# A decoder layer on one core: the up half is built in the fourth product's bank, the late splits come one plain unit later, and the bank copies have an earlier place in the queue

## The chip, the core and the metric

The kernel runs on one core of one Trainium2 chip. TensorE multiplies matrices into the eight banks of PSUM, ScalarE and VectorE work on PSUM and on SBUF, GpSimd (POOL) starts software DMAs here, among them those that add to what lies at the target, and SyncE (SP) starts plain loads. Each engine takes its instructions in the order of its queue; semaphores make one engine wait for another. The metric is the device time of one launch in microseconds, the median of several runs.

## The reference

One layer of a hybrid decoder for 256 tokens, width 2048, in float32: a half-step SwiGLU, a mixer (differential attention and a matrix-memory LSTM after one combined projection), an output projection, a second half-step SwiGLU, and a final RMSNorm. Nearly all of the work is in the weight products:

```python
def swiglu(h, w_gate, w_up, w_down):
    return (jax.nn.silu(h @ w_gate) * (h @ w_up)) @ w_down
...
x = x + 0.5 * swiglu(rmsnorm(x, ffn1_norm[l]), ffn1_w_gate[l], ffn1_w_up[l], ffn1_w_down[l])
h = rmsnorm(x, mix_norm[l])
a_q, a_k, a_v, m_q, m_k, m_v, m_o, m_i, m_f = jnp.split(h @ w_in[l], split_idx, axis=-1)
...
x = x + jnp.concatenate([y_a, y_b], axis=-1) @ w_out[l]
x = x + 0.5 * swiglu(rmsnorm(x, ffn2_norm[l]), ffn2_w_gate[l], ffn2_w_up[l], ffn2_w_down[l])
```

The inner width of each SwiGLU is 5632. All weights come from HBM once, 393 MB of reads.

## The kernel before, in words

**Float32 by three products.** A weight tile is split on ScalarE into a rounded part (`hi`, a cast, L131) and on VectorE into the rest (`lo`, a subtraction that follows the cast, L132). The activations are split in the same way beforehand. A product is then three matmuls (`mms`): L173 and L174 with the high weights, L176 with the low ones. The split tiles lie in a ring of four pairs of buffers (pool `wsp`, `bufs=4`). One entry in the list `splits` is one unit: mostly two 128-row blocks of weights, that is six or twelve matmuls.

**Pairs.** Two column chunks of 512 columns are worked through together by the class `Paired`: `wa` and `wb`, which for the FFN are gate and up of the same chunk, and elsewhere two neighbouring chunks. The result has four banks: two halves of the tokens times two chunks. The inner dimension goes in blocks of 256 rows. The first `ns` blocks of a pair use a scheme of Strassen's kind with seven products of 128 x 128 x 512 in place of eight; the others are plain units (`plain`). There are 45 pairs: `ns` is 5 in the FFN's gate and up chunks (2 in the first pair of all), 3 or 1 in the down chunks, 2 for the first projection pair, 3, 4, 4, 4, 3 in the mixer and 3 in the output projection.

**One pair, in order of its products.** `leading` loads three weight blocks per block (`raw`), multiplies A1 into the bank `self.x`, copies that bank to the seeded bank N11 (L444, through `copied`), adds weight blocks on VectorE (L448), multiplies S1 into the bank `self.d`, and then adds `raw[2]` to `raw[0]`, by a DMA from POOL (L455), or on VectorE where `by_dma` is false (L457), as in the down chunks. `sums` copies `self.d` to SBUF (`ds`, L488), multiplies S2 onto `self.x`, starts a DMA that adds another weight block to `raw[0]` (L494), copies `self.x` to the seeded bank N12 (L495), multiplies the first late weights (`bare`) into N11, multiplies S3 onto `self.x`, copies it to the seeded bank N21 (L499), and on VectorE turns N12 and `self.x` into `ds` minus themselves (L502). The copies of L495 and L499 run on ScalarE as L464; TensorE may go on writing into `self.x` only when the copy has read it. `second` works through the plain units of `wa` into N11 and N21, and after each plain unit one late split (`both`): of `raw[0]` and `raw[2]`, with the products B2 into N21 and S4 into N12. Its banks are then evacuated as the first chunk. `third` runs the plain units of `wb` into N12 and `self.x`, in turn with the next pair's `leading` (`Chain.run`).

**What sets the order.** A planner orders each engine's queue by priority and by what it expects to be ready. Weight splits have priority `AHEAD`, copies and evacuations 40 more (`soon`). Beside that, `ahead_of_splits(i, ins)` puts an instruction into a list, and `split_weights` makes the split that comes `SLACK` = 4 units later follow it on ScalarE (list 0) or VectorE (list 1). That is a bound: the copy can stand earlier, not later. The weight loads of the next pair reuse the `raw` buffers (pool `wr`, five) once the late splits have read them; plain and late units load through five buffers of their own (`rawp`) on SP.

**Banks.** PSUM has eight: three in the ring `acc` (`bank()`, also used by the mixer's small products), three seeded (N11, N12, N21), two for transposes.

Of the kernel before, what the change touches and what calls it, by code (L numbers as in the profile page):

```python
# [21 lines left out]
KD = D // P  # L22
# [30 lines left out]
SEEDED = N11, N12, N21 = "n11", "n12", "n21"  # L53
# [6 lines left out]
def tile_trunk_layer(ctx: ExitStack, tc: tile.TileContext, x, xt, par, bias_if, lamv, fnorm,  # L60
# [10 lines left out]
    ps_acc = ctx.enter_context(tc.tile_pool(name="ps_acc", bufs=3, space=PSUM))  # L71
# [24 lines left out]
    def seeded(which):  # L96
        return ps_acc.tile([P, CW], F32, tag=f"acc{which}", name=nm(f"acc{which}"), bufs=1)
# [46 lines left out]
    def ahead_of_splits(i, ins):  # L144
        queued[i].append((len(splits), ins))

    def split_weights(src, hi, lo):
        made = split(src, hi, lo)
        for late, q in zip(made, queued):
            while q and len(splits) >= q[0][0] + SLACK:  # L150
                after(late, q.pop(0)[1])
        return made
# [237 lines left out]
    class Paired:  # L390

        def __init__(self, xp, wa, wb, nk, ns, w0=0, queue=nc.gpsimd, by_dma=True):

            self.queue, self.by_dma = queue, by_dma
# [40 lines left out]
        def leading(self):  # L435
# [3 lines left out]
            for js in self.twos:  # L439
# [3 lines left out]
                if js[-1] == self.ns - 1:  # L443
                    self.n11 = self.copied(N11)  # L444
# [15 lines left out]
        def copied(self, which):  # L460

            t = seeded(which)[:, 0:self.n]
            with soon():
                ahead_of_splits(0, nc.scalar.copy(t, self.x))  # L464
            return t
# [18 lines left out]
        def sums(self):  # L484

            with soon():
                ds = wk("ds")[:, 0:self.n]
                ahead_of_splits(0, nc.scalar.copy(ds, self.d))  # L488
# [6 lines left out]
            self.n12 = self.copied(N12)  # L495
# [3 lines left out]
            self.n21 = self.copied(N21)  # L499
            with soon():  # L500
                for t in (self.n12, self.x):
                    ahead_of_splits(1, nc.vector.tensor_tensor(out=t, in0=ds, in1=t, op=ALU.subtract))  # L502
# [14 lines left out]
        def second(self):  # L517

            def both(j):
                t = self.split_two([self.raws[j][:, 0:3:2, :]])  # L520
                mms([self.job(self.n21, j, B2, t, 0, False, False, True), self.job(self.n12, j, S4, t, 1, False, False, True)])

            for i in range(max(self.ns, len(self.rest))):
# [6 lines left out]
                if i < self.ns:  # L530
                    both(i)
# [18 lines left out]
        def accs(self):  # L550
            return [p[:, self.off:] for p in (self.n12, self.x)]
# [40 lines left out]
    def ffn(chain, xp, rstd, wg, wu, wd, finish, first=None):  # L592
# [21 lines left out]
        for part, (n, ns) in enumerate(zip(PARTS, NP_DOWN)):  # L614
            hid = {}
            for c in range(n):
                half, end = inner(hid, c, ns)
                if done + c == 0 and first is not None:
# [3 lines left out]
                    stream = units(au, xp, wu[0], KD, banks=[functools.partial(seeded, N12), bank])  # L622
# [588 lines left out]
```

## Time and profile before

| What | Value |
|---|---|
| median of 3 runs | 1818.47 us (1815.88 to 1821.22) |
| profiled execution, its own time | 1818.1 us |
| its span, first to last instruction | 1816.4 us |
| mean granted TensorE clock | 0.997 |
| DMA packets | 443.22 MB, mean 244 GB/s |

The profile shows one execution. A row of the timeline has the start in us from the beginning of the span, the duration, the engine, the line of the kernel, the operation, what it writes and reads, and in brackets how long the engine had been idle and what released it. PE stands for TensorE's matmuls, PEld for its weight loads, ACT for ScalarE, DVE for VectorE. A row of the list of waits has the waiting group, the one that released it, the idle time in all, the number of waits and the longest. A row of the groups has, after the bar, busy time and mean duration in ns, then the idle time before and its releasers. A row of the stretches has, for each stretch, the busy time of PE, PEld, DVE, ACT and POOL with the number of instructions, the granted clock, the DMA share and GB/s.

### The profile page before, as it was taken

What the parts mean: (1) busy time and instruction counts of PE and PEld (TensorE: products, weight loads), DVE (VectorE), ACT (ScalarE), POOL (GpSimd) and SP (SyncE); (2) the same over time, 40 slices, a digit from 0 to 9 for tenths busy, and PEclk for the clock granted to TensorE, in tenths of its full rate; (3) what the DMA queues carried; (4) which work ended last, traced back from release to release, by engine and by line L of the source; (5) the groups of instructions that cost most, each with busy time, mean ns of one, the idle gap of its engine ahead of it and who ended that gap; (6) DMA issues with size and microseconds to landing.
All of it is one profiled execution on the core that took longest, in us unless ns stands there. A gap on an engine that the chain in (4) does not pass through costs nothing. (4 is left out here: it accounts for less than half of the span.)

```text
span 1816.4 us, 24465 instructions
## 1 busy us (share of the span) xinstructions
PE 1772.5 (98%) x7955; PEld 1443.7 (79%) x7955; DVE 1560.5 (86%) x2074; ACT 1261.0 (69%) x1939; POOL 471.1 (26%) x669
## 2 busy tenths in 40 slices
PE   9899999999999999999999999999999999999997
PEld 7688778788887887987788788788788788878886
DVE  6788888889988989796788899899887889988997
ACT  7566766767676767677576777776776767676765
POOL 0031431333243322112222112131432333143310
PEclk9999999999999999999999999999999999999999
DMA  9887998999899986687877678997998999899974
GB/s 337 249 212 229 249 265 269 216 282 259 270 241 270 264 279 197 183 258 208 232 208 208 169 228 225 240 277 240 255 274 271 240 275 265 240 261 278 259 256 122
DMA packets 161857, 443.22 MB, mean 244 GB/s; under 512 B 18273, under 2 KB 19585, under 8 KB 161473
## 3 DMA queue, kind: packets, MB, share of 16 engines
q0 software_dynamic: 82256, 204.67, 47.6%
q1 hardware_dynamic: 78464, 234.90, 36.8%
q10 hardware_dynamic: 1008, 2.09, 0.3%
q8 instruction: 62, 1.02, 0.2%
q14 instruction: 67, 0.54, 0.1%
HBM read 393.48 MB, written 2.10 MB: 218 GB/s over the span
## 5 line engine op out<-in xcount | busy, mean ns | idle before, releaser
L131 ACT CAST wh<-raw 128x512 fp32r<-128x512 f32 (+1 forms) x845 | 568.9, 705 | 307.2 <-DVE raw L448 144.2
L132 DVE TENSOR_TENSOR wl<-raw,wh 128x512 fp32r<-128x512 f32 (+1 forms) x845 | 646.9, 793 | 112.8 <-ACT wh L131 97.6
L132 DVE TENSOR_TENSOR wl<-rawp,wh 128x1024 fp32r<-128x1024 f32 (+3 forms) x324 | 387.6, 1199 | 81.6 <-ACT wh L131 78.7
L131 ACT CAST wh<-rawp 128x1024 fp32r<-128x1024 f32 (+3 forms) x324 | 334.0, 1033 | 112.3 <-PE accn L174 59.0
L173 PE MATMUL accn<-wh,xt 128*128 128x512 f32 (+2 forms) x888 | 350.5, 397 | 2.1 <-ACT accn L464 1.3
L174 PE MATMUL accn<-wh,xt 128*128 128x512 f32 (+2 forms) x888 | 343.7, 389 | 0.0
L173 PE MATMUL acc<-wh,xs 128*128 128x512 f32 (+2 forms) x712 | 280.0, 394 | 28.3 <-ACT accn L464 21.4
L174 PE MATMUL acc<-wh,xs 128*128 128x512 f32 (+2 forms) x712 | 275.6, 388 | 0.0
L176 PE MATMUL accn<-wl,xt 128*128 128x512 f32 (+2 forms) x888 | 258.0, 389 | 0.2
L176 PE MATMUL acc<-wl,xs 128*128 128x512 f32 (+2 forms) x712 | 233.0, 388 | 0.0
L455 POOL DMA_DIRECT2D raw<-raw x128 | 110.8, 873 | 465.6 <-DVE wl L132 379.2
L173 PE MATMUL accn<-wh,xs 128*128 128x512 f32 (+1 forms) x576 | 225.8, 393 | 2.7 <-ACT wh L131 2.3
L174 PE MATMUL accn<-wh,xs 128*128 128x512 f32 (+1 forms) x576 | 223.9, 390 | 0.0
L448 DVE TENSOR_TENSOR raw<-raw 128x1024 f32<-128x1024 f32 x168 | 199.7, 1216 | 0.4
L173 PEld LDWEIGHTS accn<-wh,xt 128*128 128x128 f32 x888 | 166.1, 188 | 42.0 <-ACT accn L464 5.6
L176 PEld LDWEIGHTS accn<-wl,xt 128*128 128x128 f32 x888 | 165.9, 188 | 37.2 <-DVE wl L132 3.5
L174 PEld LDWEIGHTS accn<-wh,xt 128*128 128x128 f32 x888 | 166.8, 188 | 31.8
L173 PEld LDWEIGHTS acc<-wh,xs 128*128 128x128 f32 x712 | 133.8, 188 | 70.3 <-ACT accn L464 34.9
L176 PE MATMUL accn<-wl,xs 128*128 128x512 f32 (+1 forms) x576 | 182.6, 390 | 0.7 <-DVE wl L132 0.5
L176 PEld LDWEIGHTS acc<-wl,xs 128*128 128x128 f32 x712 | 133.1, 188 | 31.4 <-DVE wl L132 3.8
L174 PEld LDWEIGHTS acc<-wh,xs 128*128 128x128 f32 x712 | 133.9, 188 | 25.9 <-DVE xs L132 0.4
L173 PEld LDWEIGHTS accn<-wh,xs 128*128 128x128 f32 x576 | 108.7, 189 | 26.6 <-ACT wh L131 3.2
(236 smaller groups left out, 2112.7 us busy)
## 6 DMA issues: line engine op xcount, KB each, us to landing
rawp<-in_wd_dram SPq DMA_DIRECT2D x96, 512.0 KB, 5.5
raw<-in_wg_dram POOLq DMA_DIRECT2D x182, 256.0 KB, 7.2
raw<-in_wu_dram POOLq DMA_DIRECT2D x80, 512.0 KB, 8.6
rawp<-in_wu_dram SPq DMA_DIRECT2D x74, 512.0 KB, 6.6
rawp<-in_wg_dram SPq DMA_DIRECT2D x70, 512.0 KB, 5.6
raw<-raw POOLq DMA_DIRECT2D x126, 256.0 KB, 4.1
rawp<-in_win_dram SPq DMA_DIRECT2D x44, 512.0 KB, 5.6
late<-in_wg_dram SPq DMA_DIRECT2D x41, 512.0 KB, 9.6
```

The source lines that it names most:

```text
L131: return (nc.scalar.copy(hi, src), nc.vector.tensor_tensor(out=lo, in0=src, in1=hi.bitcast(F32), op=ALU.subtract))
L132: nc.vector.tensor_tensor(out=lo, in0=src, in1=hi.bitcast(F32), op=ALU.subtract))
L173: nc.tensor.matmul(acc, lh, rh, start=first, stop=False, skip_group_check=on)
L174: nc.tensor.matmul(acc, ll, rh, start=False, stop=False, skip_group_check=on)
L176: nc.tensor.matmul(acc, lh, rl, start=False, stop=last, skip_group_check=on)
L448: nc.vector.tensor_tensor(out=raw[:, 0:2, :], in0=raw[:, 0:3:2, :], in1=raw[:, 1:2, :].to_broadcast([P, 2, n]), op=ALU.add)
L455: nc.gpsimd.dma_start(raw[:, 0, :], raw[:, 2, :], accum_op=ALU.add)
```

## The change

The seeded bank N12 is dropped and the ring `acc` gets a fourth bank. In `sums` the second copy of `self.x` goes to an SBUF tile (`us`), and VectorE subtracts it at once from `self.d`, in place; `self.d` is then what N12 was, for S4 and for the plain units of `wb`. The copies made by `copied` (N11, `ds`, `us`, N21) get a bound of three units instead of four. In `second` the late split of a block comes after the plain unit that follows, not after its own, so the loop has up to one more turn. Pairs with up to three blocks add `raw[2]` on VectorE instead of by DMA. The first chunk's up half takes both banks from the ring.

```diff
-SEEDED = N11, N12, N21 = "n11", "n12", "n21"
+SEEDED = N11, N21 = "n11", "n21"
...
-    ps_acc = ctx.enter_context(tc.tile_pool(name="ps_acc", bufs=3, space=PSUM))
+    ps_acc = ctx.enter_context(tc.tile_pool(name="ps_acc", bufs=4, space=PSUM))
...
-    def ahead_of_splits(i, ins):
-        queued[i].append((len(splits), ins))
+    def ahead_of_splits(i, ins, slack=SLACK):
+        queued[i].append((len(splits) + slack, ins))
...
-            while q and len(splits) >= q[0][0] + SLACK:
+            while q and len(splits) >= q[0][0]:
...
-            self.queue, self.by_dma = queue, by_dma
+            self.queue, self.by_dma = queue, by_dma and ns > 3
...
-                    self.n11 = self.copied(N11)
+                    self.n11 = self.copied(self.x, seeded(N11))
...
-        def copied(self, which):
-            t = seeded(which)[:, 0:self.n]
+        def copied(self, src, t):
+            t = t[:, 0:self.n]
             with soon():
-                ahead_of_splits(0, nc.scalar.copy(t, self.x))
+                ahead_of_splits(0, nc.scalar.copy(t, src), SLACK - 1)
             return t
...
-            with soon():
-                ds = wk("ds")[:, 0:self.n]
-                ahead_of_splits(0, nc.scalar.copy(ds, self.d))
+            ds = self.copied(self.d, wk("ds"))
...
-            self.n12 = self.copied(N12)
+            us = self.copied(self.x, wk("us"))
+            with soon():
+                ahead_of_splits(1, nc.vector.tensor_tensor(out=self.d, in0=self.d, in1=us, op=ALU.subtract))
...
-            self.n21 = self.copied(N21)
+            self.n21 = self.copied(self.x, seeded(N21))
             with soon():
-                for t in (self.n12, self.x):
-                    ahead_of_splits(1, nc.vector.tensor_tensor(out=t, in0=ds, in1=t, op=ALU.subtract))
+                ahead_of_splits(1, nc.vector.tensor_tensor(out=self.x, in0=ds, in1=self.x, op=ALU.subtract))
...
-            for i in range(max(self.ns, len(self.rest))):
+            for i in range(max(self.ns + 1, len(self.rest))):
...
-                if i < self.ns:
-                    both(i)
+                if 0 < i <= self.ns:
+                    both(i - 1)
...
-            return [p[:, self.off:] for p in (self.n12, self.x)]
+            return [p[:, self.off:] for p in (self.d, self.x)]
...
-                    stream = units(au, xp, wu[0], KD, banks=[functools.partial(seeded, N12), bank])
+                    stream = units(au, xp, wu[0], KD, banks=[bank, bank])
```

More of the change, by code (lines that the diff above doesn't have):

```diff
@@ L520, in both @@
                 t = self.split_two([self.raws[j][:, 0:3:2, :]])
-                mms([self.job(self.n21, j, B2, t, 0, False, False, True), self.job(self.n12, j, S4, t, 1, False, False, True)])
-            for i in range(max(self.ns, len(self.rest))):
+                mms([self.job(self.n21, j, B2, t, 0, False, False, True), self.job(self.d, j, S4, t, 1, False, False, True)])
+            for i in range(max(self.ns + 1, len(self.rest))):
                 aside(side)
```

## The prediction

> **What bounds the kernel now.** I read the page first, then the list of who waited for whom on the matmul queue, then that list by stage, then the ScalarE and matmul timelines around single waits.
>
> ```profile
> span 1816.4 us, 24465 instructions
> ```
> ```profile
> PE 1772.5 (98%) x7955; PEld 1443.7 (79%) x7955; DVE 1560.5 (86%) x2074; ACT 1261.0 (69%) x1939; POOL 471.1 (26%) x669
> ```
> ```profile
> PE acc L173 <- ACT accn L464: 21.4, 27, 2.5
> ```
> ```profile
> PE accn L173 <- ACT accn L464: 1.7, 4, 0.6
> ```
>
> TensorE is the bound: it is busy for 98% of the span and idle for 1816.4 - 1772.5 = 43.9 us. The change leaves its matmuls as they are (one start-up matmul fewer, while the first weights are still on their way), so only idle time can go. Most of that has one cause: L464, the ScalarE copy of a product's bank, lets TensorE go on only after 21.4 + 1.7 = 23.1 us of idle time in 31 waits. The idle figure is a little short. Rows of matmuls overlap:
>
> ```profile
> 225.40 0.50 PE L173 MATMUL acc<-wh,xs 128*128 128x512 f32 x1 [1.53 <-ACT accn L464]
> 225.74 0.40 PE L174 MATMUL acc<-wh,xs 128*128 128x512 f32 x1
> 225.97 0.39 PE L173 MATMUL acc<-wh,xs 128*128 128x512 f32 x1
> ```
>
> In step, a matmul starts 0.23 us after the one before (225.74, 225.97), though its row is 0.39 long. A wait therefore costs its idle time plus about 0.16 us. By stage, each row from its own stretch (48 to 73 us, 73 to 690, 690 to 740, 740 to 1090, 1090 to the end):
>
> ```profile
> PE acc L173 <- ACT wh L131: 3.9, 2, 2.6
> PE acc L173 <- ACT accn L464: 2.5, 1, 2.5
> ```
> ```profile
> PE acc L173 <- ACT accn L464: 6.8, 9, 1.5
> ```
> ```profile
> PE accn L173 <- ACT accn L464: 1.3, 3, 0.6
> ```
> ```profile
> PE acc L173 <- ACT accn L464: 1.8, 2, 0.9
> ```
> ```profile
> PE acc L173 <- ACT accn L464: 4.2, 6, 1.5
> ```
> ```profile
> PE acc L173 <- ACT accn L464: 6.2, 9, 1.4
> ```
>
> **Copies ahead in the queue, and the order of the late splits.** A copy waits for its turn on ScalarE. Its bound is the fourth unit split after its place in the program; now it is the third. With four weight buffers, the third cannot start before the last unit that feeds the copy has been read, so a copy in front of it holds ScalarE for a few tenths of a us at most, and the split it passes is needed two or three units later (a unit of six matmuls is 6 x 0.23 = 1.36 us). I cost that delay at nothing; with no cover it is one copy, 0.58 us, per pair. What a copy gains depends on what stood before it. Three kinds, ScalarE rows. Five blocks in the middle of an FFN stage, the copy behind the casts of all five S3 blocks:
>
> ```profile
> 394.98 2.70 ACT L131 CAST wh<-raw 128x512 fp32r<-128x512 f32 x5
> 397.58 0.58 ACT L464 COPY accn<-acc 128x512 f32<-128x512 f32 x1
> ```
>
> It passes the fifth cast and starts 0.52 us earlier (2.70 for five, overlapped). Four blocks in the mixer, where it passes a whole late unit, about 0.95 us:
>
> ```profile
> 929.04 1.05 ACT L131 CAST wh<-late 128x1024 fp32r<-128x1024 f32 x1
> 929.99 0.59 ACT L464 COPY accn<-acc 128x512 f32<-128x512 f32 x1
> ```
>
> Three, two or one block, where it stands behind a late split that itself waits for the accumulating DMA:
>
> ```profile
> 157.05 1.05 ACT L131 CAST wh<-raw 128x1024 fp32r<-128x1024 f32 x1 [0.90 <-DMA raw<-in_wd_dram]
> 158.01 1.04 ACT L131 CAST wh<-rawp 128x1024 fp32r<-128x1024 f32 x1
> 158.96 0.58 ACT L464 COPY accn<-acc 128x512 f32<-128x512 f32 x1
> ```
>
> Here the change in `second` helps as well: the plain unit now comes before that late split, and the bound of three lets the copy go before it; 0.90 + 1.0 us are gained, more than the stall. A fourth kind gains nothing: after a down stage the copy already stands before S3's fifth cast, so the new bound does not bind.
>
> ```profile
> 354.48 2.20 ACT L131 CAST wh<-raw 128x512 fp32r<-128x512 f32 x4
> 356.56 0.60 ACT L464 COPY accn<-acc 128x512 f32<-128x512 f32 x1
> ```
> ```profile
> 1630.58 0.50 PE L173 MATMUL acc<-wh,xs 128*128 128x512 f32 x1 [1.17 <-ACT accn L464]
> ```
>
> ```profile
> 439.96 0.50 PE L173 MATMUL acc<-wh,xs 128*128 128x512 f32 x1 [0.28 <-ACT accn L464]
> ```
>
> ```profile
> 830.29 0.50 PE L173 MATMUL acc<-wh,xs 128*128 128x512 f32 x1 [0.26 <-ACT accn L464]
> ```
>
> There are six long ones, the first at 225.40, the last at 1630.58, about 7.3 us of idle time together, and four short ones of 0.28, the first at 439.96; the row at 830.29 is of a four-block pair of the mixer. The sum by stage, idle time plus 0.16 a wait:
>
> - FFN stages (73 to 690, 1090 to the end): 6.8 + 1.3 + 6.2 = 14.3 us idle; less 0.8 for the last pair (below), 7.3 for the six, 1.1 for the four and 0.6 left of one stall longer than its shift: 4.5, and 0.16 for each of the ten waits that are left = **6.1 us** gone.
> - Mixer (740 to 1090): 4.2 + 0.16 x 6 = 5.2 us. Two four-block stalls lose 0.95 each, a third goes whole (0.26 + 0.16); the three-block ones stay, since their copy already precedes the new bound: **2.3 us** gone.
> - 690 to 740: the two-block pair, whose copy stands behind a late split, loses its stall, half of 1.8 and 0.16; the other stays: **1.0 us**.
>
> **The up half in the fourth product's bank.** The copy `us` now goes to SBUF, and the subtraction writes into `self.d`. Copies keep their number (four a pair) and VectorE its subtractions (two a pair).
>
> ```profile
> L464 ACT COPY accn<-acc 128x512 f32<-128x512 f32 x132 | 76.6, 581 | 7.7 <-PE acc L176 5.4 <-DVE xres L1154 2.3
> ```
> ```profile
> L488 ACT COPY ds<-acc 128x512 f32<-128x512 f32 x44 | 25.5, 579 | 1.3 <-PE acc L176 1.2
> ```
>
> The copy to PSUM takes 581 ns, the copy of such a bank to SBUF 579: no difference. The Trainium skill speaks against this part: "ScalarE: Activation LUTs", section "Step-by-step: what each stage is for", says that ScalarE writes to PSUM faster than to SBUF. By that rule the 45 copies would grow and their waits with them, but it gives no figure, and this trace does not agree, 581 against 579.
>
> The earlier subtraction holds up only VectorE's fourth split behind it, which needs a later cast anyway; the S4 matmuls that read its result come several units later. What goes is a wait for a bank: the copy into N12 had to wait until the end of the previous pair had read that bank, which shows once.
>
> ```profile
> 1784.44 0.57 ACT L464 COPY accn<-acc 128x512 f32<-128x512 f32 x1 [2.31 <-DVE xres L1154]
> ```
>
> The last pair's stall goes with it: 0.8 + 0.16 = **1.0 us**. Banks stay at eight, and during `second` two of the four `acc` banks are free, as before two of three.
>
> **VectorE in place of the DMA for up to three blocks.** Sixteen accumulations (2 + 2 + 3 + 3 + 3 + 3 blocks) leave the POOL queue and become adds of 0.69 us:
>
> ```profile
> L457 DVE TENSOR_TENSOR raw<-raw 128x512 f32<-128x512 f32 x40 | 27.4, 690 | 0.8
> ```
>
> In the mixer they lie beside TensorE. From 690 to 740 VectorE is full, and I charge the two adds there in full, **+1.1 us** (narrower blocks).
>
> ```profile
> 690.00:740.00 50.00, 48.05 (x236) 40.57 (x235) 48.14 (x78) 41.85 (x76) 12.14 (x18) 1.00 0.74 211
> ```
>
> The big effect is on the first pair:
>
> ```profile
> 61.07 1.14 ACT L131 CAST wh<-raw 128x512 fp32r<-128x512 f32 x2 [3.27 <-DMA raw<-raw]
> ```
> ```profile
> 65.19 1.04 ACT L131 CAST wh<-raw 128x1024 fp32r<-128x1024 f32 x1 [2.02 <-DMA raw<-in_wg_dram]
> 66.14 0.58 ACT L464 COPY accn<-acc 128x512 f32<-128x512 f32 x1
> ```
> ```profile
> 70.20 1.05 ACT L131 CAST wh<-raw 128x1024 fp32r<-128x1024 f32 x1 [2.50 <-DMA raw<-in_wg_dram]
> 71.15 0.58 ACT L464 COPY accn<-acc 128x512 f32<-128x512 f32 x1
> ```
>
> ScalarE waits 3.27 us for the accumulating DMA, then the first copy stands behind a late split that waits 2.02 us, the second behind one that waits 2.50. TensorE's idle time here is 2.6 + 2.5 and a little. Afterwards the sum is made on VectorE right behind the low half that reads the old value, the wait of 3.27 us goes, and the first copy goes before the second plain unit. What is late next is the second copy: its bound is now behind the first late split, whose data still land at 65.2. So it runs at about 66.2 instead of 71.15: **5.0 us** gone. If the planner puts it before that split as well, up to 3 us more.
>
> **What the new order of late splits can cost.** The plain units in front of them load on SP into buffers that were freed five splits before, so their turn one late unit (1.36 us) earlier costs nothing. But each late split frees a buffer into which the next pair loads, on POOL, in order. The second is now split two units later than the one it trades places with, 2.7 us. I follow the second load:
>
> ```profile
> 366.46 0.55 POOL L413 DMA_DIRECT2D raw<-in_wg_dram  x1 [1.74 <-DVE wl L132]
> ```
> ```profile
> raw<-in_wg_dram POOLq DMA_DIRECT2D x182, 256.0 KB, 7.2
> ```
> ```profile
> 374.82 1.14 ACT L131 CAST wh<-raw 128x512 fp32r<-128x512 f32 x2 [0.30 <-PE accn L174]
> ```
> ```profile
> 380.51 0.39 PE L173 MATMUL acc<-wh,xs 128*128 128x512 f32 x1
> ```
>
> It lands at 373.7 and is cast second, at 375.3: 1.6 us of slack, so 2.7 us make it 1.1 late. TensorE needs it at 380.51, over 4 us after the cast. The delay is covered, but the cover gets thin. Four late units now follow the last plain one instead of three, on a VectorE that is 86% busy. For both I charge **+2 us**, between nothing and the rival below.
>
> **Sum.** -5.0 - 6.1 - 2.3 - 1.0 - 1.0 + 1.1 + 2.0 = -12.3 us. The profiled execution took 1818.1 us, 1.7 more than its span, close to the median of 1818.47. Forecast: 1818.1 - 12.3 = **1805.8 us**. A measurement tells about 0.3%, 5.5 us, from no change.
>
> **Rivals.**
>
> - *More than forecast*, about 1796: the planner, whose order shifts as a whole, also moves the copies after the down stages (six stalls, 7.3 + 1.0 us), and part of the further 3 us of the first pair comes too: 1805.8 - 8.3 - 1.5. For it: those stalls have the same shape. Against it: nothing there binds them. Chance 0.10.
> - *The change does not do what it says*, about 1815: ScalarE's order stays, because most copies already stand where the planner wants them, or the low half on VectorE, which follows each cast, ends the same waits. Then the first pair's 5.0 and the last pair's 1.0 remain, less 3.1 of cost: -2.9 us. Chance 0.14.
> - *Slower*, about 1834: the next pair's load takes the copy's place. For it: 1.6 us of slack against a shift of 2.7. Against it: the 4 us of cover. It decides the sign once TensorE waits over 12.3 / 20 = 0.6 us in each of the 20 five-block pairs; at 1.4 us it is +28, and 1818.1 - 12.3 + 28 = 1833.8. Chance 0.10.
>
> **The numbers.** The forecast's own case has 0.66, with 1800 to 1811 as its own range: 6.1 + 2.3 taken half or whole, the first pair 3 to 8. Faster 0.66 + 0.10 = 0.76, same 0.14, slower 0.10. The range from 1796 to 1819 reaches over the first two rivals and leaves out the third and the edges.
>
> **What would show it.** In the list of waits, TensorE behind copies falls from 23.1 us to about 12; the stalls near 225, 357 and 545 us stay, those near 398, 586 and 930 shrink or go; near 61 us no wait for the accumulating DMA, near 66 one wait instead of three. The forecast is wrong if waits of the product L173 for first-block casts (L131, released by a load) appear before each five-block pair, or if VectorE's L132 becomes what TensorE waits for.

## The result, and the profile after

The changed kernel takes 1792.17 us (median of 4 runs, 1790.12 to 1795.30) where the kernel before takes 1818.03 on the same chip: a ratio of 0.9858, with a 95% interval from 0.9837 to 0.9879, or 25.9 us less. The forecast was 1805.8 with a range from 1796 to 1819: the sign is right, the gain is a bit more than twice what was forecast, and the time lies below the range. The profiled execution of after is the slowest of its four (1795.3 us).

The page of after, span and busy times:

```profile
span 1793.6 us, 24405 instructions
```
```profile
PE 1767.8 (99%) x7954; PEld 1442.5 (80%) x7954; DVE 1565.4 (87%) x2090; ACT 1263.8 (70%) x1939; POOL 458.3 (26%) x653
```

TensorE's idle time fell from 43.9 to 1793.6 - 1767.8 = 25.8 us. The matrix of who waits for whom on the matmul queue of after (group, releaser, us in all, times, longest):

```profile
PE acc L173 <- ACT us L464: 4.6, 5, 1.7
PE acc L173 <- ACT wh L131: 2.8, 5, 1.2
PE accn L173 <- ACT wh L131: 2.1, 3, 1.1
PE accn L173 <- ACT accn L464: 1.3, 1, 1.3
```

Waits behind copies fell from 23.1 us in 31 waits to 4.6 + 1.3 = 5.9 us in 6, where about 12 were forecast. The same list of after for the two FFN stages (66 to 667 us, 1068 to 1795), its rows of copies:

```profile
PE acc L173 <- ACT us L464: 0.8, 1, 0.8
```
```profile
PE acc L173 <- ACT us L464: 1.5, 2, 1.2
```

Before, these stages had 6.8 + 1.3 + 6.2 = 14.3 us of such idle time. The forecast left 9.0 of it (7.3 for the six long stalls, 1.1 for the four short ones, 0.6); 2.3 are left. Where the time went by stage follows from the starts of the same matmul in both traces, counted from the end. Each figure is how much sooner after gets through the stage:

| Stage (us of before) | forecast | profiled executions |
|---|---|---|
| up to 48 | 0 | 1.6 |
| first pair, 48 to 92 | 5.0 | 6.3 |
| FFN stages, 92 to 690 and 1090 to 1790 | 6.1 + 1.0 - 2.0 = 5.1 | 8.8 + 6.0 = 14.8 |
| 690 to 740 | 1.0 - 1.1 = -0.1 | 1.9 |
| mixer, 740 to 1090 | 2.3 | -0.3 |
| after the last matmuls | 0 | -1.5 |
| sum | 12.3 | 22.8 |

So the FFN stages hold most of the surprise. (The 1.6 us of the start come and go between kernels with the first loads. The 1.5 lost after the last matmuls are lost, give or take 0.4, in every kernel with adds on VectorE past the first pair, and in no other; why was not followed. The first pair's 6.3 and the mixer's -0.3 each hold a stretch at half the pace, 1.8 us in before and 1.6 us in after; the experiments and the last section come to it.) In the first pair ScalarE's order is as it was described. Its timeline of after:

```profile
58.48 0.59 ACT L464 COPY us<-acc 128x512 f32<-128x512 f32 x1 [0.76 <-PE acc L176]
58.96 1.05 ACT L131 CAST wh<-rawp 128x1024 fp32r<-128x1024 f32 x1
61.80 1.04 ACT L131 CAST wh<-raw 128x1024 fp32r<-128x1024 f32 x1 [1.79 <-DMA raw<-in_wg_dram]
62.76 0.58 ACT L464 COPY accn<-acc 128x512 f32<-128x512 f32 x1
```

The copy `us` goes when TensorE has ended the products that it reads (0.76 us of waiting for L176). The copy into N21 stands behind the first late split, as forecast, and that split still waits for its load, but the load has landed at 61.8 instead of 65.2 (1.6 of the difference are the start's).

After the three-block down pairs, where the forecast saw no gain, the second copy of before, then of after:

```profile
222.20 0.58 ACT L488 COPY ds<-acc 128x512 f32<-128x512 f32 x1
222.67 2.19 ACT L131 CAST wh<-raw 128x512 fp32r<-128x512 f32 x4
224.75 0.59 ACT L464 COPY accn<-acc 128x512 f32<-128x512 f32 x1
```
```profile
211.90 0.58 ACT L464 COPY ds<-acc 128x512 f32<-128x512 f32 x1
212.37 1.06 ACT L131 CAST wh<-late 128x1024 fp32r<-128x1024 f32 x1
213.31 1.67 ACT L131 CAST wh<-raw 128x512 fp32r<-128x512 f32 x3
214.87 0.59 ACT L464 COPY us<-acc 128x512 f32<-128x512 f32 x1
```

Three S3 casts stand ahead of it where four stood before, and the first late cast, which stood ahead of `ds` at 220.78, stands behind it. After the one-block down pairs it is still four, and a stall is left:

```profile
340.37 2.20 ACT L131 CAST wh<-raw 128x512 fp32r<-128x512 f32 x4
342.46 0.60 ACT L464 COPY us<-acc 128x512 f32<-128x512 f32 x1
```
```profile
343.11 0.50 PE L173 MATMUL acc<-wh,xs 128*128 128x512 f32 x1 [0.84 <-ACT us L464]
```

### The profile page after: what moved, and what is told of

Its sections match the earlier page's. It is cut to its first block, busy times and chain, and to the rows that moved or that the text cites. A ratio compares the mean times of both kernels' runs of the same rounds, so it can differ in the third digit from the quotient of the medians.

```text
span 1793.6 us, 24405 instructions
## 1 busy us (share of the span) xinstructions
PE 1767.8 (99%) x7954; PEld 1442.5 (80%) x7954; DVE 1565.4 (87%) x2090; ACT 1263.8 (70%) x1939; POOL 458.3 (26%) x653
## 5 line engine op out<-in xcount | busy, mean ns | idle before, releaser
L173 PE MATMUL acc<-wh,xs 128*128 128x512 f32 (+2 forms) x904 | 353.2, 391 | 7.4 <-ACT us L464 4.6
L174 PE MATMUL acc<-wh,xs 128*128 128x512 f32 (+2 forms) x904 | 350.3, 388 | 1.0 <-DVE xs L132 1.0
L176 PE MATMUL acc<-wl,xs 128*128 128x512 f32 (+2 forms) x904 | 304.5, 389 | 0.1
L173 PE MATMUL acc<-wh,xt 128*128 128x512 f32 (+2 forms) x608 | 235.1, 387 | 0.2 <-ACT wh L131 0.2
L174 PE MATMUL acc<-wh,xt 128*128 128x512 f32 (+2 forms) x608 | 234.0, 386 | 0.0
L173 PE MATMUL accn<-wh,xt 128*128 128x512 f32 (+1 forms) x592 | 232.7, 396 | 0.0
L174 PE MATMUL accn<-wh,xt 128*128 128x512 f32 (+1 forms) x592 | 228.4, 389 | 0.0
L173 PEld LDWEIGHTS acc<-wh,xs 128*128 128x128 f32 x904 | 170.0, 188 | 48.9 <-ACT us L464 11.5
L176 PEld LDWEIGHTS acc<-wl,xs 128*128 128x128 f32 x904 | 169.2, 188 | 39.6 <-DVE wl L132 5.0
L448 DVE TENSOR_TENSOR raw<-raw 128x1024 f32<-128x1024 f32 x168 | 199.5, 1215 | 0.3
L174 PEld LDWEIGHTS acc<-wh,xs 128*128 128x128 f32 x904 | 170.1, 188 | 35.1 <-DVE xs L132 2.1
L176 PE MATMUL acc<-wl,xt 128*128 128x512 f32 (+2 forms) x608 | 170.6, 388 | 0.3
L176 PE MATMUL accn<-wl,xt 128*128 128x512 f32 (+1 forms) x592 | 166.2, 388 | 0.0
L173 PE MATMUL accn<-wh,xs 128*128 128x512 f32 (+1 forms) x384 | 151.1, 394 | 3.7 <-ACT wh L131 2.1
L174 PE MATMUL accn<-wh,xs 128*128 128x512 f32 (+1 forms) x384 | 148.7, 388 | 0.0
L176 PE MATMUL accn<-wl,xs 128*128 128x512 f32 (+1 forms) x384 | 133.8, 390 | 0.3
L176 PEld LDWEIGHTS acc<-wl,xt 128*128 128x128 f32 x608 | 112.0, 188 | 27.5 <-DVE wl L132 6.0
```

The source lines that it names most:

```text
L173: nc.tensor.matmul(acc, lh, rh, start=first, stop=False, skip_group_check=on)
L174: nc.tensor.matmul(acc, ll, rh, start=False, stop=False, skip_group_check=on)
L176: nc.tensor.matmul(acc, lh, rl, start=False, stop=last, skip_group_check=on)
L448: nc.vector.tensor_tensor(out=raw[:, 0:2, :], in0=raw[:, 0:3:2, :], in1=raw[:, 1:2, :].to_broadcast([P, 2, n]), op=ALU.add)
```

## The experiments

The change has four parts, and three theories were set against each other. **A**, the forecast's: the bound of the copies and the order of the late splits move the copies, the adds help the first pair, the bank does little. **B**: the seeded bank N12, which the previous pair still reads, had held the second copy, and dropping it gives most. **C**: the later late splits cost time. Each ratio below is to the kernel before on the same chip, with its interval; "us" is 1818 times the difference.

### One part at a time

The bound alone, e1:

```diff
-    def ahead_of_splits(i, ins):
-        queued[i].append((len(splits), ins))
+    def ahead_of_splits(i, ins, slack=SLACK):
+        queued[i].append((len(splits) + slack, ins))
...
-                ahead_of_splits(0, nc.scalar.copy(t, self.x))
+                ahead_of_splits(0, nc.scalar.copy(t, self.x), SLACK - 1)
...
-                ahead_of_splits(0, nc.scalar.copy(ds, self.d))
+                ahead_of_splits(0, nc.scalar.copy(ds, self.d), SLACK - 1)
```

> The kernel before with the bound of the copies of `copied` and of `ds` at three units, nothing else. Theory A (the forecast's: the bound and the order of the late splits move the copies ahead): the mid-stage five-block stalls shrink by 0.5 us each and two of the mixer's go, 5 to 8 us less, about 1811; the six long stalls behind the copies after down stages (225 us and so on) stay. Theory B (the bank: the planner lets the copy into N12 come late because N12 is still being read by the previous pair; its own place, not the bound, was what was late): 1 to 3 us less, about 1816, and stalls behind copies stay above 18 us. First pair: no change in either, since its adds are still made by DMA.

The late splits alone, e2:

```diff
-            for i in range(max(self.ns, len(self.rest))):
+            for i in range(max(self.ns + 1, len(self.rest))):
...
-                if i < self.ns:
-                    both(i)
+                if 0 < i <= self.ns:
+                    both(i - 1)
```

> The kernel before with the late splits one plain unit later, nothing else. Theory A: one to three-block pairs gain, the first pair's copies go ahead of the late split that waits 2.0 and 2.5 us for its data: 3 to 6 us less, about 1814. Theory B: no change within 3 us, about 1817. Theory C (the later late splits free the weight buffers later, and that costs): 1820 or more, with waits of the product L173 for first-block casts.

The adds alone, e3:

```diff
-            self.queue, self.by_dma = queue, by_dma
+            self.queue, self.by_dma = queue, by_dma and ns > 3
```

> The kernel before with the add of raw[2] on VectorE for pairs of up to three blocks, nothing else. Theory A: in the first pair the wait of 3.27 us for the accumulating DMA goes, but the copies still stand behind late splits that wait for their loads, so 0 to 3 us less; 690 to 740 us gets 1 us longer: about 1817. Theory D (the adds alone make the first pair's gain): 5 to 6 us less, about 1812, with TensorE's first 90 us shorter by that.

The bank alone, e4 (the copies keep the bound of four):

```diff
-SEEDED = N11, N12, N21 = "n11", "n12", "n21"
+SEEDED = N11, N21 = "n11", "n21"
...
-            self.n12 = self.copied(N12)
+            us = self.copied(self.x, wk("us"))
+            with soon():
+                ahead_of_splits(1, nc.vector.tensor_tensor(out=self.d, in0=self.d, in1=us, op=ALU.subtract))
...
-            return [p[:, self.off:] for p in (self.n12, self.x)]
+            return [p[:, self.off:] for p in (self.d, self.x)]
```

> The kernel before with the second copy into SBUF, the up half made in the fourth product's bank and N12 dropped for a fourth bank of the ring; bound of four units, late splits and adds as before. Theory A: only the wait at the end of the last pair goes, 1 us less, about 1817, and stalls behind copies stay near 22 us. Theory B: the second copy no longer waits for the previous pair to have read N12, so the planner puts it after three S3 casts where it stood behind four or five: four of the six long stalls go and most of the mid-stage ones, 8 to 14 us less, about 1807.

Then the changed kernel with one part undone, by the same edits backwards:

> The changed kernel with the bound of its copies back at four units. Theory A: 4 to 8 us slower than the changed kernel, about 1798, with mid-stage stalls behind the copies back. Theory B: within 2 us of the changed kernel, 1791 to 1795; copies stand where they did.

> The changed kernel with each late split again right after the plain unit of its own block. Theory A: 2 to 6 us slower, about 1796, the first pair among it (its copies again behind late splits that wait for data). Theory B: within 2 us. Theory C (later late splits cost): 1 to 3 us faster than the changed kernel.

> The changed kernel with the adds of raw[2] by DMA in all gate and up pairs and the mixer's, as before. Theory A: the first pair's 3.27 us wait is back, 5 to 6 us slower, about 1798. If the order of the copies alone made the first pair's gain: 0 to 3 us slower, about 1794.

> The changed kernel with the second copy again into the seeded bank N12 and three banks in the ring; bound, late splits and adds as changed. Theory A: 1 to 2 us slower than the changed kernel, about 1794. Theory B: the six long stalls come back and more, 8 to 14 us slower, about 1803, which would be near the forecast.

| Part | alone | us | changed kernel without it | us lost against 0.9858 |
|---|---|---|---|---|
| bound | 0.9962 (0.9947 to 0.9977) | -6.9 | 0.9904 (0.9890 to 0.9918) | 8.4 |
| late splits | 0.9952 (0.9936 to 0.9967) | -8.7 | 0.9890 (0.9875 to 0.9905) | 5.8 |
| adds | 0.9974 (0.9962 to 0.9986) | -4.7 | 0.9916 (0.9903 to 0.9930) | 10.5 |
| bank | 1.0025 (1.0012 to 1.0038) | +4.5 | 0.9878 (0.9865 to 0.9890) | 3.6 |

**Theory B falls**: without the bank 22.2 of 25.8 us stay, and the bank alone is slower. (The 3.6 us of the last row are not clear of the noise: 0.9878 and 0.9858 have intervals that overlap.) Its own profile shows where:

```profile
730.12 0.70 PE L173 MATMUL acc<-wh,xs 128*128 128x392 f32 x1 [2.75 <-ACT us L464]
```
```profile
932.97 0.50 PE L173 MATMUL acc<-wh,xs 128*128 128x512 f32 x1 [3.09 <-ACT us L464]
```

Two copies, in the first projection and in the mixer, hold TensorE up for some 3 us each, where before they did for about 1. **Theory C falls** too: the late splits alone are 8.7 us faster, and the changed kernel without them is 5.8 slower. What they cost is counted with the forecast's charge for them, below.

And the parts need each other: alone they sum to -15.8 us, together they give -25.8. The profiled executions show it in two places. From 690 to 740 us no part alone brings more than 0.9 us, and all together 1.9. In the second FFN stage (1090 to the end) TensorE's idle time behind copies is 6.2 us before, 6.9, 3.5, 8.1 and 6.6 us with the bound, the late splits, the adds or the bank alone, and 1.5 after. The first pair is another case (extra time from 48 to 92 us, start to start beyond the usual step, worked out from the matmul rows; the rest is what the long waits and the half pace leave):

| us | before | e1 bound | e2 late splits | e3 adds | e8 these three | after |
|---|---|---|---|---|---|---|
| all | 9.9 | 8.2 | 8.5 | 8.8 | 5.7 | 3.6 |
| long waits from 57 us on | 5.9 | 3.4 | 3.6 | 4.1 | 1.9 | 1.5 |
| half pace behind them, about | 1.8 | 2.6 | 2.7 | 2.5 | 1.6 | 0 |
| rest, two waits near 51 us above all | 2.2 | 2.2 | 2.2 | 2.2 | 2.2 | 2.1 |

Behind a long wait matmuls can go on at half their pace for a time, 0.43 us from start to start; before shows it from 67.15 us on:

```profile
67.15 0.63 PE L174 MATMUL acc<-wh,xs 128*128 128x512 f32 x1
67.58 0.63 PE L173 MATMUL acc<-wh,xs 128*128 128x512 f32 x1
```

So each part alone takes 1.8 to 2.5 us off the waits and all together 4.4, less than their sum; but one long wait is left with one part alone, and the half pace behind it is longer than before. With the bound alone (first row) the copies are out of the way, and TensorE waits for a cast that waits for the accumulating DMA; with the adds alone (second row) that DMA is gone, and the copy stands behind the late split that waits for its load:

```profile
62.66 0.79 PE L173 MATMUL acc<-wh,xs 128*128 128x512 f32 x1 [3.26 <-ACT wh L131]
```
```profile
65.44 0.80 PE L173 MATMUL acc<-wh,xs 128*128 128x512 f32 x1 [3.93 <-ACT accn L464]
```

The stall after each second copy, pair by pair, tells the parts apart in the FFN (us by which the matmul behind the copy starts late; a dash is under 0.2):

| us of before | before | e1 bound | e2 late splits | e3 adds | e4 bank | after |
|---|---|---|---|---|---|---|
| 225, 545, 1314, 1630: after three-block down pairs | 1.3 to 1.7 | 1.7 | 0.22 | 1.3 to 1.7 | 1.3 to 1.7 | 0.22 |
| 357, 1442: after one-block down pairs | 1.2, 1.2 | 0.7, 1.2 | 0.7, 1.5 | 1.7, 0.7 | 0.7, 0.7 | 1.0, 1.3 |
| 304: a one-block down pair | 1.2 | - | - | 1.2 | 1.2 | - |
| 398, 586, 1354, 1671: the second five-block pair after a down stage | 0.3 | - | 0.3 | 0.3 | 0.3 to 0.6 | - |
| 439, 628, 1524, 1713: the third | 0.4 to 0.5 | 0.5 | - | 0.4 to 0.5 | 0.4 to 0.5 | - |
| 1784: the last pair | 1.0 | 1.5 | 1.0 | 1.0 | - | - |

Four rows answer to one part each; that of 304 goes with the bound or with the late splits, and that of 357 and 1442 follows none. The bound moves what it was said to move (the row of 0.3). The last pair's stall is the bank's: it goes with the bank alone and stays in e8, which has the other three parts (1.60 us of idle time at 1761.90). But the four long stalls and the four of 439 go with the late splits alone, which the forecast had credited with nothing there.

### Which pair's late splits

The kernel before with the late splits one unit later in the down pairs alone (e11), or in all others (e12):

```diff
-            for i in range(max(self.ns, len(self.rest))):
+            d = 1 if not self.by_dma else 0
+            for i in range(max(self.ns + d, len(self.rest))):
...
-                if i < self.ns:
-                    both(i)
+                if d <= i < self.ns + d:
+                    both(i - d)
```

e12 has `if self.by_dma` (down pairs are made with `by_dma=False`).

> The kernel before with the late splits one plain unit later in the down pairs alone. In the whole edit alone (1810.8) the four long stalls behind the second copy after three-block down pairs went (225, 545, 1314 and 1630 us: 1.3 to 1.7 us each). Theory down: the late order of the down pair in front frees its weight buffers later, so the planner casts one S3 block fewer ahead of the next pair's copy: all four go here, to 0.22 each, and the mid-stage 0.4 of 439, 628, 1524 and 1713 us stay: 5 us less, about 1814. Theory own: it is the pair's own order behind its copy that moves it; then those four stay and the time is that of before.

> The kernel before with the late splits one plain unit later in all pairs but the down pairs. Theory down: the four long stalls after three-block down pairs stay at 1.3 to 1.7 us, the 0.4 at 439, 628, 1524 and 1713 us go, and 716 us has the wait for VectorE's subtraction of about 2 us: 3 to 4 us less, about 1816. Theory own: the four long stalls go here, to 0.22: about 1811.

e11: 0.9963 (0.9949 to 0.9977); all four long stalls fall to 0.22, and 0.4 stays at 439 and its like. e12: 1.0001 (0.9983 to 1.0019); the four stay at 1.4 to 1.7, those of 439 go. So theory "down" holds: **the order in one pair moves the copy of the next**. ScalarE at the same place, e12 first, then e11:

```profile
217.50 1.04 ACT L131 CAST wh<-late 128x1024 fp32r<-128x1024 f32 x1
218.44 0.60 ACT L324 ACTIVATE part<-acc 128x512 f32<-128x512 f32 x1
218.92 0.59 ACT L488 COPY ds<-acc 128x512 f32<-128x512 f32 x1
219.39 2.19 ACT L131 CAST wh<-raw 128x512 fp32r<-128x512 f32 x4
221.46 0.61 ACT L464 COPY accn<-acc 128x512 f32<-128x512 f32 x1
```
```profile
220.16 0.58 ACT L488 COPY ds<-acc 128x512 f32<-128x512 f32 x1
220.62 1.06 ACT L131 CAST wh<-late 128x1024 fp32r<-128x1024 f32 x1
221.57 1.67 ACT L131 CAST wh<-raw 128x512 fp32r<-128x512 f32 x3
223.13 0.59 ACT L464 COPY accn<-acc 128x512 f32<-128x512 f32 x1
```

In e12 the first late cast goes early, so TensorE is through with its products by the time it needs the bank, while the copy stands behind four casts. In e11 the late cast comes after `ds`, its products cover the copy, and one S3 cast less stands in front. That the planner counts the weight buffers of the down pair as free later, and so orders the casts in this way, is argued and not shown; no run tests it. e12 alone also shows what the later splits can cost without the rest: 3.4 us of waiting behind a copy at 305 us ate its gains.

### Which adds

All adds by DMA cost the changed kernel 10.5 us, where the forecast had about 4 for them (most of the first pair's 5.0, less 1.1). e9 keeps VectorE's adds in the first pair alone (its edit is shown), e10 everywhere but there (the same line with the adds of all gate and up pairs by DMA):

```diff
-            self.queue, self.by_dma = queue, by_dma and ns > 3
+            self.queue, self.by_dma = queue, by_dma
...
-                    chain.run(Paired(xp, wg[done + c], wu[done + c], KD, np_, queue=queue), half, end)
+                    chain.run(Paired(xp, wg[done + c], wu[done + c], KD, np_, queue=queue, by_dma=np_ > 3), half, end)
```

> The changed kernel with the adds of raw[2] on VectorE only in the gate and up pair of two blocks at the start; the two-block pair at 700 us and the three-block pairs of the mixer and the output projection add by DMA again. All adds by DMA again cost the changed kernel some 11 us (1803.6 against 1792.2). Theory first: the first pair and the wait for an accumulating DMA near 258 us, which is there in every profiled kernel with the first pair's adds by DMA and in none without, carry most of it: about 1795, with no wait of 1.9 us near 258. Theory later: the waits from 690 to 860 us (2.9 us for a VectorE subtraction, 1.3 for copies and casts) carry most of it: about 1800. The forecast (VectorE is full from 690 to 740, the adds there cost 1.1 us) would have it 1 us faster than the changed kernel, 1791.

> The changed kernel with the adds of raw[2] by DMA in all gate and up pairs, the first among them, and on VectorE in the other pairs of up to three blocks. Theory first: about 1800, with the wait of 1.9 us near 258 and the long one for the first pair's casts back. Theory later: about 1795, and no subtraction awaited for 2.9 us near 716.

e9: 0.9885 (0.9866 to 0.9904), e10: 0.9879 (0.9861 to 0.9897). Both theories were half right: from 0.9916 without any, each half brings 5.6 and 6.7 us, and both together 10.5. (The intervals of e9 and e10 overlap that of the changed kernel, so by the times alone the second half is not clear of the noise. In the profiled executions e9 takes 4.3 us longer than after from 690 to 740, and e10 4.7 us longer in the first pair; part of either is half pace.) The first pair's two adds carry a second effect at a distance: where they are DMAs, the next accumulating DMAs near 260 us land late and TensorE waits. The row of before, then of e10; e9 has none there:

```profile
265.76 0.50 PE L173 MATMUL acc<-wh,xs 128*128 128x512 f32 x1 [1.64 <-ACT wh L131]
```
```profile
260.61 0.50 PE L173 MATMUL acc<-wh,xs 128*128 128x512 f32 x1 [1.64 <-ACT wh L131]
```

Why two DMAs less at 60 us make the later ones land in time stays open. The later adds matter from 690 us on. VectorE of e9, then the matmul that waits for it:

```profile
708.14 0.43 DVE L711 TENSOR_TENSOR lv<-lv 128x256 f32<-128x256 f32 x1 [2.65 <-DMA lv<-in_lamv_dram]
708.48 1.22 DVE L132 TENSOR_TENSOR wl<-rawp,wh 128x1024 fp32r<-128x1024 f32 x1
```
```profile
709.75 1.22 PE L176 MATMUL acc<-wl,xt 128*128 128x512 f32 x2 [2.59 <-DVE wl L132]
```

A small product of the mixer's (`lv`, L711) stands at the head of VectorE's queue and waits for its load, and a weight subtraction waits behind it. With the adds on VectorE the planner puts `lv` some 10 us later. e13 keeps the adds on the DMA and moves that op alone:

```diff
+    lvm = nc.vector.tensor_tensor(out=lv[:, 0:2, :], in0=lv[:, 0:2, :], in1=lv[:, 2:4, :], op=ALU.mult)
+    after(lvm, splits[-1][1])
```

(in place of L711 to L718, behind the run of the first projection pair).

> The changed kernel with all adds of raw[2] in gate, up, mixer and output pairs by DMA again, and the product of the lambda vectors (lv, L711, which waits some 2.7 us for its load ahead of a weight subtraction on VectorE) made to follow the last split of the first projection pair. The same kernel without the second part was 0.9916 of the time before, about 1803. Theory queue: the wait at 716 us (2.9 us and, in some profiles, 1.6 us more of matmuls at half the pace) is that op's: it goes, 3 to 4 us less, about 1799.5. Theory DMA: the subtraction is late because of the accumulating DMA itself; the wait stays and so does the time, about 1803.

0.9926 (0.9908 to 0.9944): no gain over e7's 0.9916, so the queue's head alone was not what cost the time. The wait for `lv` has gone, but ScalarE then shows the next thing that is late:

```profile
715.89 0.52 ACT L131 CAST wh<-raw 128x392 fp32r<-128x392 f32 x1 [1.36 <-DMA raw<-raw]
718.20 0.52 ACT L131 CAST wh<-raw 128x392 fp32r<-128x392 f32 x1 [1.78 <-DMA raw<-raw]
```

Its copy `us` follows at 723.73, and TensorE waits 2.1 us for it. So the accumulating DMA holds this stage up by itself as well, and both have to go.

### Further in the same direction

e14 sets the bound to two units, e15 makes every add on VectorE, e16 both:

```diff
-                ahead_of_splits(0, nc.scalar.copy(t, src), SLACK - 1)
+                ahead_of_splits(0, nc.scalar.copy(t, src), SLACK - 2)
...
-            self.queue, self.by_dma = queue, by_dma and ns > 3
+            self.queue, self.by_dma = queue, False
```

> The changed kernel with the bound of its copies at two units. By its queue the second copy then stands behind three S3 casts at 343 and 1420 us where it stands behind four, and behind three in the mixer's four-block pairs where it stands behind four and five. Theory casts: those four stalls shrink to 0.2 to 0.7 us, waits of TensorE behind copies fall from 5.9 to under 3 us, 2 to 4 us less than the changed kernel, about 1789. Theory cost: a copy that stands so early holds ScalarE until TensorE has ended the products that it reads, and the casts behind it are late: as the changed kernel or slower, 1792 to 1797, with waits for casts (L131) in place of copies.

> The changed kernel with every add of raw[2] on VectorE, 112 more at 0.69 us, 77 us more on a VectorE that is busy for 1565 of 1794. Theory covered: the adds lie beside TensorE, the accumulating DMAs of five-block pairs go and with them what their landing holds up: 0 to 3 us less, about 1791. Theory full: VectorE becomes what TensorE waits for (L132 behind L457) in the five-block pairs, 0.3 us or more in each of 20: 6 us more, about 1798.

> Both: bound of two units and every add on VectorE. The sum of the two theories that gain: about 1788; of the two that cost: 1800 or more.

e14: 0.9865 (0.9848 to 0.9882), no better than after. e15: 1.0086 (1.0068 to 1.0104), e16: 1.0168 (1.0147 to 1.0189), 41 and 56 us worse than after; for e15 that is far beyond either theory. In e15 the waits are for casts, 33.7 us in 24, and a pair of five blocks shows why (VectorE, then TensorE):

```profile
1153.43 1.29 DVE L457 TENSOR_TENSOR raw<-raw 128x512 f32<-128x512 f32 x2
1154.63 1.23 DVE L448 TENSOR_TENSOR raw<-raw 128x1024 f32<-128x1024 f32 x1
```
```profile
1156.56 0.50 PE L173 MATMUL acc<-wh,xs 128*128 128x512 f32 x1 [2.49 <-ACT wh L131]
```

Two adds stand ahead of the sum (L448) that the last S1 cast waits for. VectorE is busy for 89% of e15's span and for 9.28 of the 10 us from 1150 on, so it is nearly full there: the rows show what its queue's order delays, and that its load plays no part is not shown. In e14 the first pair's copies no longer stall, but VectorE waits 2.39 us for `lv` at 713.70 and TensorE 2.13 us behind it. e17 moves `lv` as in e13 under the bound of two, e18 in the changed kernel:

> The changed kernel with the bound of its copies at two units and the product of the lambda vectors made to follow the last split of the first projection pair. Theory queue head: the wait of 2.3 us at 716 us of the kernel with the bound alone (0.9865 of before) is that op's and goes, while the first pair's copies keep their 1.6 us and the pairs after one-block down pairs their 0.2 to 0.8: 0.984 to 0.985 of before, faster than the changed kernel (0.9858). Theory cost: what stands late there is the second copy or the casts, as it was with the adds on the DMA; another wait of 1 to 2 us takes its place: 0.986 to 0.987.

> The changed kernel with the product of the lambda vectors made to follow the last split of the first projection pair, and nothing else. Both theories: its VectorE shows no wait for that load, so nothing goes: 0.985 to 0.987 of before, within 2 us of the changed kernel. If it is 3 us or more faster, the wait is there in most executions and the profiled one missed it.

e17: 0.9848 (0.9834 to 0.9861), 1791.49 us (1789.59 to 1793.52); e18: 0.9866 (0.9852 to 0.9879), 1795.24 us (1793.49 to 1796.63). e17 is the fastest of all, by 3.75 us over e18 on the same chip, and e18 is as the changed kernel. Against the changed kernel itself, 0.9848 and 0.9858 have intervals that overlap, so this is not shown to be faster than it.

## Why the prediction was right in sign and too small

**What bounds the kernel: right.** The matmuls stayed; idle time fell by 18.1 us of the span's 22.8, and 17.2 of it was behind copies. The rest is in the steps of stalled matmuls, which the forecast priced at 0.16 us a wait.

**First pair, -5.0: right in its mechanism, 1.3 short.** The adds, the bound and the late splits do it together, as it said; 6.3 in the profile. Of these 4.4 are waits, a little less than forecast, though the load of the first late split, which "still land[s] at 65.2", landed 1.8 us sooner after the start than that. The other 1.8 are the half pace from 67.15 us on, which before has here and after has not. The forecast read the waits alone and had no term for it; whether it comes is partly luck, since e9 and e18, with the same adds, bound and late splits in this pair, have it here.

**"A fourth kind gains nothing ... so the new bound does not bind": this step failed.** The sentence on the bound is true (e1 leaves these stalls at 1.7). But the step took the bound as the only thing that could move those copies, and credited the late splits in one to three-block pairs alone. The late splits of the down pair in front move the next pair's copy (e11 against e12). The four stalls after three-block down pairs lost 1.70 + 1.30 + 1.60 + 1.33 - 4 x 0.22 = 5.1 us, and the four short ones, said to stay too, about 1.8. These 6.9 us are two thirds of what was missing in the profiled execution (22.8 - 12.3 = 10.5). The pairs behind one-block down pairs stayed, as forecast.

**The charge for the later late splits, +2.0: right in size.** Waits for casts in the FFN stages went from 3.3 to 3.8 us (start to start), but 1.8 of the 3.3 are the wait near 266 us, which goes with the first pair's adds. The changed kernel without the late splits (e6) has 2.0 there, so they cost 1.8, and 0.4 more in waits for VectorE (1.8 to 2.2). None is longer than 0.9, so the cover that was called thin held for the five-block pairs. The longest is behind a down pair's load (ScalarE, then TensorE, of after):

```profile
313.86 1.04 ACT L131 CAST wh<-raw 128x1024 fp32r<-128x1024 f32 x1 [1.08 <-DMA raw<-in_wd_dram]
```
```profile
314.96 0.50 PE L173 MATMUL acc<-wh,xs 128*128 128x512 f32 x1 [0.72 <-ACT wh L131]
```

What the forecast missed is what this cost buys, the stalls of the failed step.

**The adds from 690 to 740, +1.1: wrong in sign.** "VectorE is full" was true and beside the point. The stretch got 1.9 us faster: both copies' stalls went (1.1 and 0.9 us, start to start), where the forecast let one stay, and the adds cost TensorE nothing that shows. With DMA adds (e7, e9) it was 1.1 and 2.4 us slower than before, since the casts wait for the accumulating DMA and VectorE's queue for a load. The adds in the mixer do not just "lie beside TensorE" either: by the medians the later adds are worth 4.9 us in all (0.9885 against 0.9858, with intervals that overlap), and this is after a cost, since in the kernels that have them TensorE waits for VectorE near 1000 us, in after for these:

```profile
PE tr L1041 <- DVE xt L378: 1.3, 2, 1.0
```
```profile
PE acc L174 <- DVE xs L132: 1.0, 2, 0.7
```

**Not in the sum: the wait near 266 us** (1.8 us, and about half of the copy's 1.3 us behind it). The trace of before shows it, and the forecast took no note of the accumulating DMA outside the first pair.

**Mixer, -2.3: right in size by luck.** Stalls behind copies fell from 5.1 to 2.6 us (start to start), but not where the forecast had them. The three-block pair near 978 lost its 0.9, which was said to stay, and near 930, where 0.95 was to go, the stall grew from 1.3 to 1.9. There the copy does pass the late cast, as described; the stall is 0.4 with the bound alone and 0.35 in the changed kernel without the bank (e8), so more than the bound decides it. The half pace behind that stall and new waits for VectorE then took the gain away in this execution, which lost 0.3; e17 and e18 went through the stage 2.8 and 2.2 us faster than before.

**Bank: the wait of the last pair, -1.0, right.** In the changed kernel the bank is worth 3.6 us by the medians, not clear of the noise, and alone it costs 4.5. The copy to SBUF takes about what the copy to PSUM takes, as the forecast had it: 581 to PSUM against 579 ns before, 573 against 583 after, where the 10 ns more make 0.5 us over 45 copies. The rule of the Trainium skill that the forecast cites ("ScalarE: Activation LUTs", "Step-by-step: what each stage is for"), that ScalarE writes to PSUM faster than to SBUF, shows here at most as these 10 ns. The groups of after (the means hold one or two narrower copies):

```profile
L464 ACT COPY accn<-acc 128x512 f32<-128x512 f32 (+1 forms) x90 | 51.6, 573 | 13.8 <-PE acc L176 11.7
L464 ACT COPY us<-acc 128x512 f32<-128x512 f32 (+1 forms) x45 | 26.2, 583 | 5.2 <-PE acc L176 5.1
```

**The rivals.** "More than forecast", at 1796 and with a chance of 0.10, comes nearest. It named the main thing that happened, the planner moving the copies after the down stages, though four of its six stalls went and two stayed. Its second part did not happen as told: the first pair's copy still stands behind the late split, and the surplus there is the half pace. Its reason against itself, "nothing there binds them", is the failed step again. The slower rival's mechanism, the next pair's load taking the copy's place, shows in no five-block pair; the wait near 315 us is its only like.

## What to carry to other kernels

When a planner makes the queue, an edit that changes when one pair's buffers come free can reorder the next pair: ask of each stall which instruction stands ahead of it and what would put it elsewhere, not only whether the edited bound touches it. Obstacles that stand in a row (here a DMA and a waiting product at 716 us) hide each other, so parts tried one at a time can undervalue the whole. When stages of two traces are compared, take the half pace out first: it can hide or double what a wait is worth. The adds by DMA held casts up by 1.4 to 3.3 us in the first pair and near 716 us, but putting all such adds on VectorE put them ahead of sums that ScalarE needs sooner and cost 41 us.

## What the runs showed of the hardware that was not expected

A long wait can cost more than itself. The profiled execution of after, TensorE at one pair of the mixer and the granted clock of that stretch (us, then busy times of PE, PEld, DVE, ACT and POOL, clock, DMA share, GB/s):

```profile
910.33 0.51 PE L173 MATMUL acc<-wh,xs 128*128 128x512 f32 x1 [1.72 <-ACT us L464]
910.67 0.40 PE L174 MATMUL acc<-wh,xs 128*128 128x512 f32 x1
...
912.38 0.63 PE L173 MATMUL acc<-wh,xs 128*128 128x512 f32 x1
912.81 0.63 PE L174 MATMUL acc<-wh,xs 128*128 128x512 f32 x1
```
```profile
910.00:914.00 4.00, 3.67 (x10) 2.94 (x11) 4.00 (x6) 3.11 (x4) 0.00 (x0) 0.65 0.51 168
```

From 911.5 on matmuls start 0.43 us apart instead of 0.23: half the pace, for eight matmuls, 1.6 us on top of a wait of 1.9 (start to start). The same wait of 1.89 stands at this pair in five of the kernels; in two of them, this one and e13, the half pace follows, in three it does not. Over all profiled executions the half pace followed 44 waits, all of them of about 1.7 us and more, and some 60 waits of 1.6 us and more, up to 3.3, went without. Twenty of the 44 are in e15 and e16, where they add to what their waits cost.

The Trainium skill, "TensorE: Matmul & The Clock Gate", Part 1, says that the clock falls to half after at least one idle window of about 3.4 us, in windows that run freely. The traces agree on the windows: within each trace all stretches of half clock begin at the same place of a grid of 3.413 us and last one or two steps of it in the work between. They do not agree that a whole window has to be idle. Worked out on that grid from the matmul rows (steps at full clock, from 45 us to the last matmul), TensorE was idle for over 0.54 of a step 25 times, and the half clock followed each time; of 45 steps idle for 0.44 to 0.54 it followed 19, and of those under 0.44 none. A wait of about half a step is thus charged again when it falls within one step, and goes free when it lies across two.
